# Conv block and MLP in fp32 on one core: the first stage reordered, its matmuls partly in native fp32, TensorE's order pinned, the convolution's DRAM copies issued in separate steps

## The chip, the cores and the metric

The kernel runs on one core of one Trainium2 chip. The metric is the time of one execution in device microseconds (us). Engines are called by the names of the profile: PE (TensorE matmuls), PEld (TensorE weight loads), DVE (VectorE), ACT (ScalarE), POOL (GpSimd), SP (SyncE, which here only issues DMAs). An engine works through its instructions in the order in which they were written for it; a DMA is issued by SP in the same way and then runs on 16 DMA engines.

## The reference

One decoder layer (depth 1) with batch 1, 256 positions (T), width 2048 and an MLP of width 8192, all in fp32. With 16 tiles of 128 channels:

```python
cond = silu(c)
sh1, sc1, g1, sh2, sc2, g2 = split(cond @ mod_w + mod_b, 6)      # mod_w is 2048 x 12288
h = rms_norm(x, norm1_g) * (1 + sc1) + sh1
u = h @ w_in + b_in                                              # 2048 x 4096
u = a * sigmoid(gt), a, gt = split(u, 2)
u = causal depthwise conv, 31 taps, + dw_b
y = silu(layer_norm(u)) @ w_out + b_out                          # 2048 x 2048
x = x + (1 + g1) * y
h = rms_norm(x, norm2_g) * (1 + sc2) + sh2
x = x + (1 + g2) * (square(relu(h @ w1)) @ w2)                   # 2048 x 8192 x 2048
```

## The kernel before

Activations lie with channels on the partitions, so a tile is 128 channels by 256 positions. The weights come from DRAM in blocks of 1024 KB (2048 x 128) into five buffers `raw`; each block is used once. To keep fp32 accuracy at the rate of the type `float32r`, an operand is split into `hi` (its float32r rounding, by ACT) and `lo` (the rest, by DVE or POOL). A product is then hi·hi + hi·lo in one matmul of 512 columns (the activations' hi and lo stand side by side in a tile `hl` or `u2`) and lo·hi in one of 256 columns: L189 and L190 in `mm`, 32 such pairs for an output tile pair, called a job.

The stages, in order:

1. **Start (L86 to L405).** `x` is loaded in four DMAs, squared and summed for the norm's factor `r1`.
2. **Held half (L410 to L487).** The first `HELD` = 7 output tile pairs of `w_in` are accumulated all at once, in seven PSUM banks (`held`), k-tile by k-tile. For each of the 16 k-tiles one block `first` (896 KB, three buffers) is loaded; `split_first` splits it, `first_mm` multiplies it: 14 blocks, three matmuls of 256 columns each (L439, L442, L443). Before k-tile k can be multiplied, its modulation (scale sc1 and shift sh1) must be known, which is a product of `mod_w` with silu(c). It is done in two ways. *By row*: for a group of four k-tiles, eight chunks of 1024 KB (`mod_r`) pass through TensorE (`mod_chunk`, L207, eight matmul records for a chunk), then the row is folded into columns (`mod_finish`, L254). *By column*: for one k-tile, two blocks of 1024 KB (`mod_c`) are multiplied with silu(c) (`cond`) and summed by DVE (`mod_col`, L265). `BY_COL` names the tiles by column (0 to 3 and 12 to 15), `BY_ROW` the groups by row (1 and 2: tiles 4 to 11). The order of k is 0 to 15, so column, row, row, column.
3. **In-stage (L661 to L728).** Jobs 7 to 15 are the other nine tile pairs of `w_in`. After each, `gate` makes the tile `u[i]`. The rest of the modulation goes on as row chunks between the halves of a job (L685, the numbers in `LATE_IN`). The convolution of a channel tile is done by DVE (`conv`, 31 taps, L521), or on TensorE for the tiles in `PE_TILES` (`pe_conv`, L626): there the tile u is copied to DRAM (`flatten`, L594, `flat`), read back in four shifted copies (L611, `wide`, four DMAs for a tile), and multiplied with diagonal 32 x 32 blocks, 64 matmul records for a tile. `CONV_AT` says after which job which tiles are mixed; in job 7 these are 0, 1, 2 and 3. `find_shift` (L288) needs tiles 0 and 1.
4. **Out, up and down jobs (L745 to L815).** Layer norm, `w_out` (8 jobs; `x` is loaded again in four DMAs), then four times 8 up jobs and 8 down jobs. The up jobs read `hl`, the down jobs `u2`, in a pool `mlp` at the upper end of SBUF.

The order of the work on each engine isn't written by hand: a scheduler orders each engine's instructions by its own estimate of when they are ready, and a block under `tc.issue_after(ins)` puts its instructions on `ins`'s engine behind `ins`. `urgent()` raises the priority. The loads follow the list `order`; each goes behind the one before it on SP, and `top_up` issues one more than there are free buffers, so that SP waits for a buffer with everything behind it waiting too.

Of the kernel before, what the change touches and what calls it, by code (L numbers as in the profile page):

```python
# [37 lines left out]
BY_ROW = (1, 2)  # L38
BY_COL = (0, 1, 2, 3, 12, 13, 14, 15)
# [8 lines left out]
CONV_AT = {7: (0, 1, 2, 3), 8: (4,), 9: (5, 6), 10: (7,), 11: (8, 9), 12: (11, 10), 13: (13,), 14: (12,), 15: (14,)}  # L48
SHIFT = 2
UNSHIFTED = 6  # L50
LEAD = {1: 0, 2: 8}
# [13 lines left out]
def conv_block(ctx: ExitStack, tc: tile.TileContext, x, vec, dwq, c_row, mod_r, mod_c, w_first, w_in, w_out, w1, w2, out):  # L65
# [47 lines left out]
    room = {"raw": RAW + 1, "first": FIRST + 1, "cond": 1, "x": 4}  # L113
    todo = []

    def source(key):
# [15 lines left out]
        if kind == "x":  # L132
            return x[:, 4 * key[1] : 4 * key[1] + 4, :]
# [5 lines left out]
    def top_up():  # L139
        while todo and waiting[home(todo[0])] < room[home(todo[0])]:  # L140
# [43 lines left out]
    def mm(p, c, key, acts_of, ks=range(KT)):  # L184
        halves = parts[key]
        for k in ks:
# [3 lines left out]
            nc.tensor.matmul(  # L190
# [123 lines left out]
    def pair_of(tiles, k2):  # L314
        return tiles[k2 // 2][:, 2 * (k2 % 2) : 2 * (k2 % 2) + 2, :]
# [15 lines left out]
    def modulate(k2, r, sh, sc, h):  # L331
        n = scaled(k2, r)
# [32 lines left out]
    order += [("c", 0)]  # L365
    for b in range(4):
        ks = range(4 * b, 4 * b + 4)
        if b in BY_ROW:
            order += first[b] + [("first", k) for k in ks]
        else:  # L370
            for k in ks:
                order += by_col(k) + [("first", k)]
    order += [jobs[HELD] + (c,) for c in range(2)]
    for n, job in enumerate(jobs):
        if n >= HELD and n < len(jobs) - 1:
            order += [jobs[n + 1] + (c,) for c in range(2)]
        if job == ("out", 0):
            order += [("x", i) for i in range(4)]
# [23 lines left out]
    with tc.issue_after(end.ins):  # L402
        mods([("c", 0)])
# [15 lines left out]
    def split_first(k):  # L419
        w = take(("first", k))  # L420
        first_parts[k] = []
# [9 lines left out]
    def first_mm(k):  # L431
        parts_of = first_parts.pop(k)
        m = hl[k // 2][:, k % 2, :]
        for n in range(HELD):
            for c in range(2):
                h, j = divmod(2 * n + c, HELD)
                hi, lo = parts_of[h]
                p = held[n][:, c, :]
                nc.tensor.matmul(  # L439
                    p, hi[:, j, :], m[:, 0:T], start=(k == 0 and c == 0), stop=False, skip_group_check=True  # L440
                )
                nc.tensor.matmul(p, hi[:, j, :], m[:, T : 2 * T], start=False, stop=False, skip_group_check=True)  # L442
                state["step_end"] = nc.tensor.matmul(  # L443
                    p, lo[:, j, :], m[:, 0:T], start=False, stop=(k == KT - 1), skip_group_check=True
# [4 lines left out]
    for b in range(4):  # L449
        ks = range(4 * b, 4 * b + 4)  # L450
        if b in BY_ROW:
            for _ in range(LEAD[b]):
                next(steps, None)
            for at, key in enumerate(first[b]):
                with tc.issue_after(state["step_end"].ins):
                    mods([key])
                with tc.issue_after(state["row_end"].ins):
                    for _ in range(1 + at % 2 if LEAD[b] else 2):
                        next(steps, None)
            mod_finish()  # L460
            for k2 in (2 * b, 2 * b + 1):
                modulate(k2, r1, SH1, SC1, two())
            for k in ks:
                with tc.issue_after(state["fold_end"].ins):
                    for _ in range(2):
                        next(steps, None)
                split_first(k)
            for _ in steps:
                pass
            steps = chain(*(first_mm(k) for k in ks))  # L470
            continue
        for k in ks:
            c = k % 2
            if c == 0:
                n = scaled(k // 2, r1)
                h = two()
                new_hl(k // 2)
            mods(by_col(k))
            nc.scalar.activation(
                h[:, c, :], n[:, c, :], AF.Identity, scale=amps[SC1][:, k : k + 1], bias=mcol(SH1, k)  # L480
            )
            split_act(hl[k // 2][:, c : c + 1, :], h[:, c : c + 1, :])
            split_first(k)
            for _ in steps:
                pass
            steps = first_mm(k)
    for _ in steps:  # L487
        pass
    table(AF.Sigmoid, modc[:, 0:1])
# [105 lines left out]

    def pe_conv(ct, sq=None):
        wide = cp.tile([P, 4, T + 28], F32, name="wide", bufs=2)
        if sq is not None:
            for q in range(4):
                for g in range(4):  # L600
                    dst = wide[32 * q : 32 * q + 32, g, :]
                    src = u[ct][32 * g : 32 * g + 32, q : q + T + 28]
                    if g % 2:
                        nc.vector.tensor_copy(dst, src)
                    else:
                        nc.scalar.activation(dst, src, AF.Copy)
        else:
            src = flats.pop(ct).rearrange("(g c) t -> c g t", g=4)
            with later(ct):
                for q in range(4):  # L610
                    nc.sync.dma_start(wide[32 * q : 32 * q + 32, :, :], src[:, :, q : q + T + 28])  # L611
# [256 lines left out]
```

## Time and profile before

| what | us |
|---|---|
| median of 3 runs (lowest to highest) | 1185.8 (1181.65 to 1187.3) |
| the profiled execution, its own time | 1185.32 |
| its span, first to last instruction | 1183.5 |
| PE busy in the span | 1122.4 |
| DVE, ACT, POOL busy | 744.8, 562.4, 166.1 |
| start and held half: 0 to 146 | 146 |
| in-stage: 146 to 349 | 203 |
| norm and out jobs: 349 to 469 | 120 |
| up and down jobs: 469 to 1178 | 709 |

The stages' limits are read from the timeline of PE. A busy share says only that an engine had an instruction in it; matmul records overlap, so the pitch from one start to the next says more than the length of a record. "SPq" rows are DMA issues by SP; an issue row that is merged over several DMAs includes SP's waits between them.

### The profile page before, as it was taken

The numbers are of one execution on the slowest core, as the hardware profiler recorded it, in microseconds if no ns is written. First come the engines' busy times: TensorE is split into PE (matmuls) and PEld (weight loads), VectorE is DVE, ScalarE is ACT, GpSimd is POOL, SyncE is SP. The second block draws the span as 40 slices with busy tenths as digits, with TensorE's granted clock in tenths as the row PEclk, the third lists the DMA queues.
The fourth block names the chain that finished last, engine by engine and source line by source line (L and its number), as shares of the span: only waits on it lengthen the run. The fifth ranks groups of instructions, "written<-read, shape, count | busy, mean of one in ns | idle before, by whom it ended". The sixth has DMA issues, their size and how long they took to land.

```text
span 1183.5 us, 17371 instructions
## 1 busy us (share of the span) xinstructions
PE 1122.4 (95%) x7048; PEld 931.7 (79%) x7048; DVE 744.8 (63%) x1026; ACT 562.4 (48%) x737; POOL 166.1 (14%) x106
## 2 busy tenths in 40 slices
PE   3879968999989999999999999999999999999998
PEld 3748936666647888888888888888888888888886
DVE  3736899883435886888876555555555655555553
ACT  5234522322347567765443655444555444555441
POOL 0000273664643125200000000000000000000000
PEclk8989988999999999999999999999999999999999
DMA  9998985999977984689777555655555555555630
GB/s 390 401 401 340 414 336 173 356 323 369 305 290 269 342 325 184 222 299 348 285 280 295 194 181 176 213 178 182 200 188 178 192 197 180 182 198 189 197 133 27
DMA packets 46880, 299.81 MB, mean 253 GB/s; under 512 B 5200, under 2 KB 9424, under 8 KB 13520
## 3 DMA queue, kind: packets, MB, share of 16 engines
q1 hardware_dynamic: 46512, 297.99, 68.9%
q8 instruction: 55, 0.90, 0.3%
q10 hardware_dynamic: 288, 0.71, 0.2%
q14 instruction: 25, 0.20, 0.0%
HBM read 295.70 MB, written 2.98 MB: 252 GB/s over the span
## 4 chain that ended last, share of the span: by engine, by line
PE 81%; DMA 3%; SPq 0%; ACT 0%; issue 0%; DVE 0%; POOL 0%; POOLq 0%; ACTq 0%
PE mm L189 50%; PE mm L190 26%; DMA wide<-flat 2%; PE row L207 2%; PE mm L626 2%; DMA raw<-mod_r 1%; PE row L222 0%; SPq L153 0%; PE small L288 0%; PE row L254 0%; PE mm L623 0%; PE small L567 0%; SPq L611 0%; ACT hi L173 0%; ACT sq L340 0%
## 5 line engine op out<-in xcount | busy, mean ns | idle before, releaser
L173 ACT ACTIVATE hi<-raw 128x1024 fp32r<-128x1024 f32 x324 | 342.1, 1059 | 417.3 <-PE mm L189 408.5
L189 PE MATMUL mm<-hl,hi 128*128 128x512 f32 x1504 | 529.4, 396 | 0.2 <-DVE u L639 0.2
L174 DVE TENSOR_TENSOR lo<-raw,hi 128x1024 fp32r<-128x1024 f32 x272 | 333.1, 1226 | 246.0 <-ACT hi L173 244.2
L190 PE MATMUL mm<-hl,lo 128*128 128x256 f32 x1504 | 422.7, 281 | 0.0
L189 PE MATMUL mm<-u,hi 128*128 128x512 f32 x1088 | 384.7, 397 | 0.0
L189 PEld LDWEIGHTS mm<-hl,hi 128*128 128x128 f32 x1504 | 282.2, 188 | 79.6 <-issue 12.1
L190 PE MATMUL mm<-u,lo 128*128 128x256 f32 x1088 | 306.5, 282 | 0.0
L190 PEld LDWEIGHTS mm<-hl,lo 128*128 128x128 f32 x1504 | 284.7, 189 | 5.6 <-issue 5.4
L189 PEld LDWEIGHTS mm<-u,hi 128*128 128x128 f32 x1088 | 204.2, 188 | 50.5 <-DVE small L301 0.2
L190 PEld LDWEIGHTS mm<-u,lo 128*128 128x128 f32 x1088 | 205.1, 189 | 0.0
L174 POOL TENSOR_TENSOR lo<-raw,hi 128x1024 fp32r<-128x1024 f32 x52 | 124.4, 2407 | 99.6 <-ACT hi L173 93.9
L521 DVE SCALAR_TENSOR_TENSOR acc<-u,v,acc 128x256 f32<-128x256 f32 x252 | 107.3, 485 | 2.4
L207 PE MATMUL row<-raw,cz 128*32 128x512 f32 x448 | 61.4, 634 | 16.1 <-DMA raw<-mod_r 15.6
L265 DVE SCALAR_TENSOR_TENSOR raw<-raw 128x2048 f32<-128x2048 f32 x24 | 57.5, 2397 | 14.9 <-DMA raw<-mod_c 14.9
L390 ACT ACTIVATE two<-mm 128x512 f32<-128x512 f32 (+1 forms) x74 | 42.6, 576 | 42.0 <-PE mm L190 41.5
L439 PE MATMUL mm<-hl,hi 128*128 128x256 f32 x128 | 37.4, 303 | 19.9 <-ACT hl L181 19.9
L391 DVE TENSOR_TENSOR two<-mm,two 128x512 f32<-128x512 f32 (+1 forms) x65 | 43.9, 676 | 14.8 <-ACT two L390 13.6
L428 DVE TENSOR_TENSOR lo<-first,hi 128x896 fp32r<-128x896 f32 x32 | 33.9, 1087 | 21.2 <-ACT hi L427 21.2
L439 PEld LDWEIGHTS mm<-hl,hi 128*128 128x128 f32 x128 | 25.2, 202 | 26.6 <-ACT hl L181 21.5
L182 DVE TENSOR_TENSOR u<-two,u 128x512 fp32r<-128x512 f32 x40 | 30.8, 770 | 22.9 <-ACT u L181 22.8
L427 ACT ACTIVATE hi<-first 128x896 fp32r<-128x896 f32 x32 | 28.9, 943 | 25.6 <-DMA first<-w_first 17.4
L442 PE MATMUL mm<-hl,hi 128*128 128x256 f32 x128 | 37.8, 297 | 2.2 <-DVE hl L182 2.2
(138 smaller groups left out, 727.7 us busy)
## 6 DMA issues: line engine op xcount, KB each, us to landing
raw<-w SPq DMA_DIRECT2D x128, 1024.0 KB, 4.9
raw<-mod_r SPq DMA_DIRECT2D x56, 1024.0 KB, 7.8
raw<-mod_c SPq DMA_DIRECT2D x40, 1024.0 KB, 7.3
raw<-w_in SPq DMA_DIRECT2D x18, 1024.0 KB, 8.0
raw<-w_out SPq DMA_DIRECT2D x16, 1024.0 KB, 6.5
first<-w_first SPq DMA_DIRECT2D x16, 896.0 KB, 11.4
x<-x SPq DMA_DIRECT2D x8, 512.0 KB, 7.4
wide<-flat SPq DMA_DIRECT2D x24, 142.0 KB, 9.2
```

Source lines behind the costliest of these rows:

```text
L173: nc.scalar.activation(hi, w[:, ks, :], AF.Copy)
L174: end = engine.tensor_tensor(lo, w[:, ks, :], hi.bitcast(F32), op=ALU.subtract)
L189: nc.tensor.matmul(p[:, c, :], hi[:, k % HALF, :], m, start=(k == 0), stop=(k == KT - 1))
L190: nc.tensor.matmul(p[:, c, T : 2 * T], lo[:, k % HALF, :], m[:, 0:T], start=False, stop=(k == KT - 1), skip_group_check=True,)
L207: state["row_end"] = nc.tensor.matmul(row_ps[0][32 * k : 32 * k + 32, :], cz[:, 4 * kg + k, 3 - b : 35 - b], w[:, 4 * k : 4 * k + 4, :], s ...
L265: nc.vector.scalar_tensor_tensor(w, w, 1.0, cb, op0=ALU.mult, op1=ALU.mult, accum_out=acc)
L390: nc.scalar.activation(t1, p[:, cs, T : 2 * T], AF.Copy)
L391: nc.vector.tensor_tensor(t2, p[:, cs, 0:T], t1, op=ALU.add)
L428: nc.vector.tensor_tensor(lo, w[:, js, :], hi.bitcast(F32), op=ALU.subtract)
L439: nc.tensor.matmul(p, hi[:, j, :], m[:, 0:T], start=(k == 0 and c == 0), stop=False, skip_group_check=True)
L442: nc.tensor.matmul(p, hi[:, j, :], m[:, T : 2 * T], start=False, stop=False, skip_group_check=True)
L521: nc.vector.scalar_tensor_tensor(out, s, w, acc, op0=ALU.mult, op1=ALU.add)
```

## The change

- `BY_ROW` becomes groups 0 and 1, `BY_COL` tiles 8 to 15: the held half now begins with two groups by row and ends with eight tiles by column. The loads are reordered with it: never more than three `first` blocks stand in a row, `c` is loaded behind the rows, and for tiles by column a `first` block comes one tile later.
- Tiles 8, 10, 12 and 14 (`NATIVE`) are not split: TensorE multiplies the fp32 block with the fp32 activation, one fp32 matmul in place of three.
- `LEAD`: six steps of `first_mm` ahead of the second group's chunks, then two steps behind each chunk; `scaled` is called ahead of the chunks.
- `x` is one tile: two loads at the start in place of four, one load later in place of four.
- In the in-stage the row chunks and everything of `mix` get `issue_after` the last matmul of the job so far (`mm_end`).
- The copy to DRAM, the reading back and the convolution are three steps: `flatten` in job i, `widen` in job i + 1 (for the held tiles 0 and 1 right behind the gates), `pe_conv` later. Tiles 0 and 1 move from job 7 to job 8.
- A pad of 64 floats ahead of the pool `mlp` puts `u2` 256 bytes lower.

```diff
-BY_ROW = (1, 2)
-BY_COL = (0, 1, 2, 3, 12, 13, 14, 15)
+BY_ROW = (0, 1)
+BY_COL = range(8, KT)
+NATIVE = (8, 10, 12, 14)
...
-CONV_AT = {7: (0, 1, 2, 3), 8: (4,), 9: (5, 6), ...
+CONV_AT = {7: (2, 3), 8: (0, 1, 4), 9: (5, 6), ...
...
-LEAD = {1: 0, 2: 8}
+LEAD = 6
...
-    xs = [start_pool.tile([P, 4, T], F32, name=f"x{i}") for i in range(4)]
-    for i in range(4):
-        nc.sync.dma_start(xs[i], x[:, 4 * i : 4 * i + 4, :])
+    xs = start_pool.tile([P, KT, T], F32, name="x0")
+    for i in range(2):
+        nc.sync.dma_start(xs[:, 8 * i : 8 * i + 8, :], x[:, 8 * i : 8 * i + 8, :])
...
-                raw[key] = x_pool.tile([P, 4, T], F32, name=f"x{key[1]}")
+                raw[key] = x_pool.tile([P, KT, T], F32, name="x1")
...
-    order += [("c", 0)]
-    for b in range(4):
-        ks = range(4 * b, 4 * b + 4)
-        if b in BY_ROW:
-            order += first[b] + [("first", k) for k in ks]
-        else:
-            for k in ks:
-                order += by_col(k) + [("first", k)]
+    order += first[0] + held_w(0, 1, 2) + first[1][:5] + held_w(3) + first[1][5:] + held_w(4, 5, 6) + [("c", 0)]
+    for k in BY_COL:
+        order += by_col(k) + held_w(k - 1)
+    order += held_w(KT - 1)
...
     def split_first(k):
         w = take(("first", k))
+        if k in NATIVE:
+            first_parts[k] = w
+            return
...
+                if k in NATIVE:
+                    state["step_end"] = nc.tensor.matmul(
+                        p, parts_of[:, j, :], h, start=begin, stop=end, skip_group_check=True
+                    )
+                    continue
...
+    for b in BY_ROW:
+        ks = range(4 * b, 4 * b + 4)
+        pairs = range(2 * b, 2 * b + 2)
+        if b == 0:
+            mods(first[0])
+            ns = [scaled(k2, r1) for k2 in pairs]
+        else:
+            step(LEAD)
+            ns = [scaled(k2, r1) for k2 in pairs]
             for at, key in enumerate(first[b]):
+                if at == 5:
+                    split_first(3)
+                    steps = chain(steps, first_mm(3))
                 with tc.issue_after(state["step_end"].ins):
                     mods([key])
                 with tc.issue_after(state["row_end"].ins):
+                    step(2)
+        mod_finish()
+        for k2, n in zip(pairs, ns):
+            modulate(k2, n, SH1, SC1, two())
+        if b == 0:
+            for k in range(3):
                 split_first(k)
+            steps = chain(*(first_mm(k) for k in range(3)))
+        else:
+            with tc.issue_after(state["fold_end"].ins):
+                for _ in steps:
+                    pass
+            for k in range(4, 7):
+                split_first(k)
+            steps = chain(*(first_mm(k) for k in range(4, 7)))
+    mods([("c", 0)])
+    for k in BY_COL:
...
+        split_first(k - 1)
+        steps = chain(steps, first_mm(k - 1, h_last if k > 8 else None))
+        for _ in steps:
+            pass
+        h_last = h[:, c, :]
...
+    def widen(ct):
+        wides[ct] = cp.tile([P, 4, T + 28], F32, name="wide", bufs=2)
+        src = flats.pop(ct).rearrange("(g c) t -> c g t", g=4)
+        with later(ct):
+            for q in range(4):
+                nc.sync.dma_start(wides[ct][32 * q : 32 * q + 32, :, :], src[:, :, q : q + T + 28])
...
+        for i in range(HELD):
+            if i in PE_TILES:
+                widen(i)
...
                     mm(p, c, job + (c,), hl, ks)
-                    mods(rows[:1])
+                    with tc.issue_after(state["mm_end"].ins):
+                        mods(rows[:1])
...
+            if i - 1 in flats:
+                widen(i - 1)
             if i in PE_TILES and i < KT - 1:
                 flatten(i)
             for ct in CONV_AT.get(n, ()):
-                mix(ct)
+                with tc.issue_after(state["mm_end"].ins):
+                    mix(ct)
...
+            pad = ctx.enter_context(tc.tile_pool(name="pad", bufs=1, side="right"))
+            pad.tile([P, 64], F32, name="pad")
             mp = ctx.enter_context(tc.tile_pool(name="mlp", bufs=1, side="right"))
...
-                xs = [take(("x", n)) for n in range(4)]
+                xs = take(("x", 0))
```

More of the change, by code (lines that the diff above doesn't have):

```diff
@@ L112, in conv_block @@
     waiting = {"raw": 0, "first": 0, "cond": 0, "x": 0}
-    room = {"raw": RAW + 1, "first": FIRST + 1, "cond": 1, "x": 4}
+    room = {"raw": RAW + 1, "first": FIRST + 1, "cond": 1, "x": 1}
     todo = []
@@ L189, in mm @@
             nc.tensor.matmul(p[:, c, :], hi[:, k % HALF, :], m, start=(k == 0), stop=(k == KT - 1))
-            nc.tensor.matmul(
+            state["mm_end"] = nc.tensor.matmul(
                 p[:, c, T : 2 * T], lo[:, k % HALF, :], m[:, 0:T], start=False, stop=(k == KT - 1),
@@ L314, in pair_of @@
     def pair_of(tiles, k2):
+        if tiles is xs:
+            return xs[:, 2 * k2 : 2 * k2 + 2, :]
         return tiles[k2 // 2][:, 2 * (k2 % 2) : 2 * (k2 % 2) + 2, :]
@@ L377, in conv_block @@
         if job == ("out", 0):
-            order += [("x", i) for i in range(4)]
+            order += [("x", 0)]
         order += after[job]
@@ L457, in conv_block @@
                 with tc.issue_after(state["row_end"].ins):
[L458 to L466, printed above, removed]
-                split_first(k)
-            for _ in steps:
-                pass
@@ L470, in conv_block @@
[L470 to L486, printed above, removed]
@@ L488, in conv_block @@
+    split_first(KT - 1)
+    for _ in first_mm(KT - 1, h_last):
         pass
-    table(AF.Sigmoid, modc[:, 0:1])
+    table(AF.Sigmoid, h_last[:, 0:1])
     for c in range(2):
```

70 lines of the change are left out of this document (37 added, 33 removed).

## The prediction, made before the changed kernel was run

> **What bounds the kernel now.** I read the page first: busy shares, the 40 slices, the shares of the chain that ended last.
>
> ```profile
> PE 1122.4 (95%) x7048; PEld 931.7 (79%) x7048; DVE 744.8 (63%) x1026; ACT 562.4 (48%) x737; POOL 166.1 (14%) x106
> ...
> PE   3879968999989999999999999999999999999998
> ...
> PE 81%; DMA 3%; SPq 0%; ACT 0%; issue 0%; DVE 0%; POOL 0%; POOLq 0%; ACTq 0%
> ```
>
> TensorE bounds the kernel. Its 61 us without an instruction (1183.5 − 1122.4) lie in the first 12 slices of 29.6 us, the stages that the change rewrites. The windows show what fills these stages (last two columns: share of the DMA engines, GB/s; before them TensorE's granted clock).
>
> ```profile
> 0.00:140.00 140.00, 109.83 (x799) 91.85 (x800) 82.39 (x113) 56.63 (x80) 0.92 (x6) 0.91 0.95 389
> 100.00:110.00 10.00, 10.00 (x83) 9.81 (x83) 9.21 (x13) 7.44 (x11) 0.00 (x0) 1.00 0.66 258
> 120.00:130.00 10.00, 10.00 (x86) 10.00 (x85) 9.96 (x14) 3.25 (x5) 0.00 (x0) 1.00 1.02 430
> 140.00:350.00 210.00, 190.78 (x1461) 126.24 (x1459) 141.51 (x337) 68.85 (x98) 114.69 (x69) 0.96 0.86 307
> 160.00:170.00 10.00, 2.60 (x23) 0.36 (x16) 10.00 (x26) 2.48 (x3) 8.23 (x5) 0.78 1.02 425
> 205.00:330.00 125.00, 121.80 (x875) 81.17 (x873) 77.09 (x176) 41.86 (x53) 72.00 (x32) 1.00 0.94 338
> ```
>
> Up to 140 us the DMA engines set the pace (0.95 against 1.02 when full), with a hole at 100 to 110. At 160 to 170 TensorE has work for 2.60 us; from 205 on it is full again. TensorE's timeline names the hole.
>
> ```profile
> 146.28 0.50 PE L189 MATMUL mm<-hl,hi 128*128 128x512 f32 x1 [0.23 <-DVE u L639]
> ...
> 155.55 1.06 PE L207 MATMUL row<-raw,cz 128*32 128x512 f32 x8
> ...
> 158.95 1.92 PE L207 MATMUL row<-raw,cz 128*32 128x512 f32 x16
> 161.28 1.06 PE L207 MATMUL row<-raw,cz 128*32 128x512 f32 x8 [0.40 <-DMA raw<-mod_r]
> 169.34 1.93 PE L207 MATMUL row<-raw,cz 128*32 128x512 f32 x8 [7.00 <-DMA raw<-mod_r]
> ...
> 174.21 1.87 PE L207 MATMUL row<-raw,cz 128*32 128x512 f32 x8 [0.50 <-DMA raw<-mod_r]
> 182.26 5.54 PE L626 MATMUL mm<-wide,diag 128*32 128x256 f32 x64 [6.19 <-DMA wide<-flat]
> 188.37 3.66 PE L626 MATMUL mm<-wide,diag 128*32 128x256 f32 x64 [0.57 <-DMA wide<-flat]
> 191.96 0.70 PE L288 MATMUL small<-cv,ones 128*128 128x256 f32 x2
> 192.31 0.58 PE L189 MATMUL mm<-hl,hi 128*128 128x512 f32 x1
> ```
>
> The held half ends at 146.28. Job 7's product follows, then seven row chunks (one at 155.55, two at 158.95, one at 161.28, three from 169.34 to 174.21), two convolutions, the first half of the shift, and only at 192.31 job 8's product. The scheduler had put three chunks of job 8 and both convolutions ahead of that product, and TensorE stood in front of their DMAs. The chain confirms it, and ACT's rows give the marks for the sum: the last held block in, job 7's product out, job 8's product out.
>
> ```profile
> 170.85 8.82 DMA wide<-flat
> 179.69 8.55 DMA wide<-flat
> ...
> 258.30 10.70 DMA wide<-flat
> ```
>
> ```profile
> 136.66 1.79 ACT L427 ACTIVATE hi<-first 128x896 fp32r<-128x896 f32 x2 [4.46 <-DMA first<-w_first]
> ...
> 159.06 0.60 ACT L390 ACTIVATE two<-mm 128x512 f32<-128x512 f32 x1 [5.82 <-PE mm L190]
> ...
> 205.27 0.58 ACT L390 ACTIVATE two<-mm 128x512 f32<-128x512 f32 x1
> ```
>
> **The change part by part.** *Held half, order of loads.* The bytes stay the same, so it can gain only the DMA engines' idle time: 0.07 of 136.66 us (0.95 against 1.02) is 9.6 us. The cause of much of it shows on SP; with it the pace of the held matmuls, and POOL's splits for jobs 7 and 8:
>
> ```profile
> 86.73 15.85 SPq L153 DMA_DIRECT2D first<-w_first  x4
> ...
> 155.97 0.42 SPq L594 DMA_DIRECT2D flat<-u  x1
> ...
> 170.85 2.50 SPq L611 DMA_DIRECT2D wide<-flat  x5
> ...
> 342.85 2.07 SPq L153 DMA_DIRECT2D x<-x  x4
> ```
>
> ```profile
> 143.70 16.56 POOL L174 TENSOR_TENSOR lo<-raw,hi 128x1024 fp32r<-128x1024 f32 x7
> ```
>
> ```profile
> 51.60 0.28 PE L439 MATMUL mm<-hl,hi 128*128 128x256 f32 x1
> 51.72 0.28 PE L442 MATMUL mm<-hl,hi 128*128 128x256 f32 x1
> ```
>
> Four held blocks in a row meet three buffers, and SP waits 15.85 us with the columns behind it; the hole at 100 to 110 follows. In the new order there are at most three in a row, and behind each second-group chunk (about 1 us) stand two steps of six matmuls of 0.12 us (the two starts), 2.4 us together, the pace of one 1024 KB block at 425 GB/s. I take 9.1 us of the 9.6 (bounds 0 and 9.6): nothing in the new order puts a fourth `first` block in line. What is late next is the tail: the last block, its split and its products, 146.28 − 136.66 = 9.6 us as before, since the last tile is still split. So the held half ends at 146.28 − 9.1 = 137.2.
>
> *Native fp32.* The price of a native matmul of 256 columns is in the layer norm's sums:
>
> ```profile
> 345.74 0.59 PE L583 MATMUL mm<-cv,ones 128*128 128x256 f32 x2
> 346.17 0.59 PE L584 MATMUL mm<-sq,ones 128*128 128x256 f32 x2
> ```
>
> A native one is two records and takes 0.43 us from start to start; three split ones take 3 × 0.12 = 0.36. Four tiles of 14 blocks cost 56 × 0.07 = 3.9 us more on TensorE. It is hidden: a tile by column brings 2 × 1024 + 896 KB, some 7.1 us at 425 GB/s, and its products take 5.0 or 6.0 us. Without that cover it costs the 3.9. It takes eight half-block splits off ACT and eight off DVE:
>
> ```profile
> L265 DVE SCALAR_TENSOR_TENSOR raw<-raw 128x2048 f32<-128x2048 f32 x24 | 57.5, 2397 | 14.9 <-DMA raw<-mod_c 14.9
> ...
> L428 DVE TENSOR_TENSOR lo<-first,hi 128x896 fp32r<-128x896 f32 x32 | 33.9, 1087 | 21.2 <-ACT hi L427 21.2
> ```
>
> On DVE 8 × 1.087 = 8.7 us go. A column costs DVE 2.40 us (L265), so a split tile costs 2 × 2.40 + 2 × 1.087 and some 0.8 of small work, 7.8 us, above the 7.1 of its loads, and a native one 5.6. The mean falls below the loads' pace; I count this within the 9.1.
>
> *TensorE's order and the three steps, together.* In jobs 7 and 8 TensorE's work is: two products of 11.8 us (159.06 − 146.28 less one chunk of about 1.0, the first cold pairs included), seven chunks, 7.0, two convolutions at the warm 3.66, 7.3, two sums for the shift, 0.9. Sum 38.8 us, where the timeline needed 205.27 − 146.28 = 59.0. With chunks pinned behind their own half, job 8's product no longer waits for chunks and `wide`; its weights were split by 143.70 + 16.56 = 160.3, and the splits move up with the held half. The copies have more time: `wide` is now issued behind `flat`, not behind the loads that fill 155.97 to 170.85, and is needed only after job 8's product and chunks, at 137.2 + 2 × 11.8 + 7.0 = 168, some 25 us after the gates that follow the held half. SP then waits for `flat` with the next loads behind it; up to five blocks are under way by then, which hide about 12 us of it; without them the wait falls on job 9's weights. I allow 2.1 us, near the lower of the bounds 0 and 13 (the upper one is rival (b)). Job 8's mark: 137.2 + 38.8 + 2.1 = 178.1 in place of 205.27, 27.2 us earlier. Of this 9.1 is the held half, 18.1 the in-stage.
>
> Can the DMA engines follow? From 140 to 350 they idle 0.14 × 210 = 29 us, more than 18.1. And DVE? It is busy 141.5 of these 210 us. So both have room, though the room is used up to a few us.
>
> *The rest of the in-stage.* From 205 to 330 TensorE is busy for 121.8 of 125 us: at most 3.2 us to gain, among them a wait for `wide` at 269; the pinned order may cost as much. I take 0, bounds −3.2 and +5 (a quarter us for each of 21 chunks).
>
> *`x` in fewer DMAs.* Four issues took SP 2.07 us at 342.85, one takes a quarter; the norm is being computed then, so I take 0, bounds −1.6 and +1. At the start the first half lands later, but the sums are not needed before the first group's rows are in: 0, bounds −0.5 and +1.
>
> *MLP buffers 256 bytes lower.* No work changes. The trace gives this question two rows: an up stage (reads `hl`) and a down stage (reads `u2`) with the same instructions.
>
> ```profile
> 670.00:720.00 50.00, 50.00 (x291) 44.10 (x290) 27.34 (x28) 28.24 (x35) 0.00 (x0) 1.00 0.55 190
> 770.00:820.00 50.00, 50.00 (x285) 43.43 (x284) 27.36 (x30) 20.84 (x22) 0.00 (x0) 1.00 0.55 189
> ```
>
> 291 records against 285 in 50 us, TensorE full in both: the pitch differs by 2%. So something that isn't work, possibly where the operand lies, is worth 2% of some 355 us of down jobs, 7 us. I take 0, as the sign is not known, bounds −7 (down jobs as fast as up jobs) and +7 (up jobs as slow). The Trainium skill, page "SBUF — State Buffer", section "SBUF: two separate sides", says that the engines' reads contend only at a port pair shared by VectorE and GpSimd, and that TensorE has ports of its own. By that rule the pad is worth 0, which is also my value; the two rows above don't decide it, but show that equal instructions don't always run at an equal pace.
>
> **Sum.** 9.1 + 18.1 = 27.2 us off the span of 1183.5 gives 1156.3. The profiled execution took 1185.32, 1.8 us beyond its span, so 1158.1; it stands 0.5 below the median of 1185.8. Forecast **1158 us**.
>
> **The rivals.** (a) *The held half doesn't get faster*: another wait takes the place of the four-block queue, for instance first-group products late and their chunks holding `raw`. For it: TensorE and DVE both are near the loads' pace. Then only 18.1 us go: 1167. (b) *`wide` is still late*: SP stays blocked and issues at 170 as before. Convolutions end near 192.3, but job 8's product is done by then: 205.27 − 192.3 = 13.0 us go: 1172. Against it: the issue stands earlier in SP's order. (c) *Down jobs at the up jobs' pace*: 1151. (d) *Up jobs at the down jobs' pace*: 1165. (e) *Slower: the pinned chunks*. In jobs 7 to 14 there are 28 chunks that TensorE may no longer pass. If each comes late by more than 27.2/28 = 0.97 us the gain is gone; at 1.3 us it is 36 lost, some 9 slower: 1195. For it: the DMA share of 0.94 from 205 on, and the 7.00 us wait at 169.34. Against it: chunks stand between products already there, and TensorE is full. (f) *No change*: the stalls reappear in the same sum: 1185. (g) The Trainium skill, page "DMA: Bandwidth & Descriptors", section "Where 436 GB/s comes from", gives about 358 GB/s as the memory's limit for one core. As a mechanism here: loads at 358 in place of 389 GB/s over the first 137 us would end the held half 12 us later and the kernel at 1197; the row of 120 to 130 us, 430 GB/s, is against it. Chance 0.01.
>
> **How the numbers follow.** Chances: forecast 0.41 (its own range 1152 to 1164), (a) 0.10, (b) 0.12, (c) 0.17, (d) 0.08, (e) 0.08, (f) 0.03, (g) 0.01. The range 1146 to 1175 takes in (c) less 5 and (b) plus 3, and leaves out (e), (f), (g) and their like, somewhat over 0.1. A measurement tells about 0.5% (6 us) from no change; the runs before span 0.48%. Faster: 0.41 + 0.10 + 0.12 + 0.17 + 0.08 = 0.88; same 0.03; slower 0.09.
>
> **What would show it.** Right: job 7's first L189 near 137; job 8's L189 at about 153, ahead of any L626; no wait on `wide` above 1 us before 200; job 8's product out near 178; the up and down jobs' record counts unchanged. Wrong: L207 waits of over 1 us on `mod_r` again and again between 150 and 300 (e), L626 waiting for `wide` near 168 (b), L189 near 146 (a), or a changed count for 50 us in the MLP (c, d).

## The result, and the profile after

The changed kernel takes **1166.7 us** (median of 4 runs, 1166.6 to 1168.7), against 1186.6 us of the kernel before on the same chip: a ratio of 0.984 with a 95% interval from 0.981 to 0.988. The forecast was 1158 us, its range 1146 to 1175. So the kernel got faster by about 20 us and not by 27. The profiled execution took 1166.8 us, with a span of 1164.9.

From the page of the kernel after: the busy shares, TensorE's 40 slices and the chain that ended last.

```profile
PE 1125.4 (97%) x6992; PEld 933.1 (80%) x6992; DVE 731.3 (63%) x1018; ACT 555.9 (48%) x730; POOL 167.0 (14%) x106
...
PE   5799999999989999999999999999999999999998
...
PE 84%; DVE 8%; DMA 4%; ACT 2%; issue 1%; POOL 0%; SPq 0%; ACTq 0%; DVEq 0%
```

TensorE's idle time fell from 61 to 39.5 us (1164.9 - 1125.4). The slice with a 6 (at 148 to 178 us) is gone. VectorE, which was on 0% of the chain, is now on 8% of it.

The windows say the same by stage. Columns: TensorE's matmuls, its weight loads, VectorE, ScalarE, GpSimd (busy us and count), granted clock, DMA share, GB/s.

```profile
0.00:140.00 140.00, 115.88 (x763) 95.19 (x764) 75.72 (x106) 51.10 (x74) 0.96 (x7) 0.93 0.97 397
100.00:110.00 10.00, 10.00 (x67) 9.40 (x66) 8.88 (x12) 2.39 (x5) 0.00 (x0) 1.00 0.64 252
140.00:350.00 210.00, 200.21 (x1504) 132.87 (x1503) 146.17 (x355) 85.15 (x127) 125.56 (x77) 0.98 0.91 335
160.00:170.00 10.00, 10.00 (x59) 7.80 (x58) 7.54 (x20) 4.97 (x6) 6.03 (x3) 1.00 1.01 403
205.00:330.00 125.00, 124.45 (x976) 81.48 (x979) 79.11 (x198) 44.08 (x62) 67.79 (x31) 1.00 0.91 330
```

From 160 to 170 us TensorE now works 10.00 us, before 2.60. But the hole of the DMA engines at 100 to 110 us, which the prediction meant to close, is still there (0.64).

TensorE's timeline shows where the gain is and where it isn't.

```profile
145.55 0.50 PE L190 MATMUL mm<-hl,hi 128*128 128x512 f32 x1 [1.92 <-DVE u L668]
...
175.51 3.22 PE L655 MATMUL mm<-wide,diag 128*32 128x256 f32 x54
180.49 1.07 PE L208 MATMUL row<-raw,cz 128*32 128x512 f32 x8 [1.75 <-DMA raw<-mod_r]
181.37 4.50 PE L655 MATMUL mm<-wide,diag 128*32 128x256 f32 x74
186.11 0.70 PE L289 MATMUL small<-cv,ones 128*128 128x256 f32 x2 [0.24 <-ACT cv L660]
```

Job 7's product starts at 145.55, before at 146.28: **the held half gained 0.7 us.** Its last product is through at 143.6, 2.4 us earlier than before, but TensorE then stands 1.92 us for a gate, where it stood 0.23. Then job 8's product runs ahead of both convolutions (L655 is the convolution, L626 before), and the whole set (two products, seven chunks, two convolutions, the first half of the shift) is done at about 186.5, where job 8's product, which then came last of the set, was out at 205.27. From job 7's start that is 40.9 us now and 59.0 before: **the stage of jobs 7 and 8 gained 18 us.** Of these 18.8 us in all, 18.6 arrive at the end of the span.

### The profile page after: what moved, and what is told of

Same layout as the page of the kernel before. It is cut to its first block, busy times and chain, and to the rows that moved or that the text cites. A ratio compares the mean times of both kernels' runs of the same rounds, so it can differ in the third digit from the quotient of the medians.

```text
span 1164.9 us, 17233 instructions
## 1 busy us (share of the span) xinstructions
PE 1125.4 (97%) x6992; PEld 933.1 (80%) x6992; DVE 731.3 (63%) x1018; ACT 555.9 (48%) x730; POOL 167.0 (14%) x106
## 4 chain that ended last, share of the span: by engine, by line
PE 84%; DVE 8%; DMA 4%; ACT 2%; issue 1%; POOL 0%; SPq 0%; ACTq 0%; DVEq 0%
PE mm L190 50%; PE mm L191 25%; PE row L208 3%; DVE raw L266 3%; DVE acc L542 2%; DMA wide<-flat 1%; DVE lo L430 1%; DMA first<-w_first 1%; PE small L289 1%; PE mm L655 1%; DMA raw<-w_in 1%; DMA flat<-u 1%; PE mm L450 1%; PE mm L448 1%; DMA x<-x 1%
## 5 line engine op out<-in xcount | busy, mean ns | idle before, releaser
L190 PEld LDWEIGHTS mm<-hl,hi 128*128 128x128 f32 x1504 | 282.8, 188 | 83.3 <-issue 14.1
L542 DVE SCALAR_TENSOR_TENSOR acc<-u,v,acc 128x256 f32<-128x256 f32 x252 | 102.8, 487 | 0.9
L266 DVE SCALAR_TENSOR_TENSOR raw<-raw 128x2048 f32<-128x2048 f32 x24 | 57.5, 2396 | 33.4 <-DMA raw<-mod_c 33.3
L208 PE MATMUL row<-raw,cz 128*32 128x512 f32 x448 | 60.9, 610 | 10.7 <-DMA raw<-mod_r 10.7
L392 DVE TENSOR_TENSOR two<-mm,two 128x512 f32<-128x512 f32 (+1 forms) x65 | 43.9, 676 | 14.8 <-ACT two L391 13.6
L430 DVE TENSOR_TENSOR lo<-first,hi 128x896 fp32r<-128x896 f32 x24 | 25.4, 1088 | 38.3 <-ACT hi L429 38.3
L448 PE MATMUL mm<-hl,hi 128*128 128x256 f32 x96 | 29.4, 312 | 8.7 <-ACT hl L182 8.7
L266 DVE SCALAR_TENSOR_TENSOR raw<-raw,cond 128x2048 f32<-128x2048 f32 x16 | 36.3, 2286 | 1.8 <-ACT cond L282 1.8
L208 PEld LDWEIGHTS row<-raw,cz 128*32 128x32 f32 x448 | 10.4, 109 | 30.9 <-DMA raw<-mod_r 16.5
L429 ACT ACTIVATE hi<-first 128x896 fp32r<-128x896 f32 x24 | 21.7, 940 | 17.9 <-DMA first<-w_first 16.5
```

What stands on the lines that cost most here:

```text
L190: nc.tensor.matmul(p[:, c, :], hi[:, k % HALF, :], m, start=(k == 0), stop=(k == KT - 1))
L208: state["row_end"] = nc.tensor.matmul(row_ps[0][32 * k : 32 * k + 32, :], cz[:, 4 * kg + k, 3 - b : 35 - b], w[:, 4 * k : 4 * k + 4, :], s ...
L266: nc.vector.scalar_tensor_tensor(w, w, 1.0, cb, op0=ALU.mult, op1=ALU.mult, accum_out=acc)
L392: nc.vector.tensor_tensor(t2, p[:, cs, 0:T], t1, op=ALU.add)
L430: nc.vector.tensor_tensor(lo, w[:, js, :], hi.bitcast(F32), op=ALU.subtract)
L448: nc.tensor.matmul(p, hi[:, j, :], m[:, 0:T], start=begin, stop=False, skip_group_check=True)
```

## The experiments

Each kernel was timed together with the kernel before on its chip (1184.9 to 1185.6 us); ratios are against that. First the change was taken apart.

**In-stage part alone.** The kernel before with the pins, the later place of tiles 0 and 1, and the copies in three steps.

```diff
+CONV_AT = {7: (2, 3), 8: (0, 1, 4), ...
+def widen(ct): ...            # called behind flatten
+with tc.issue_after(state["mm_end"].ins):
     mods(rows[:1])
+with tc.issue_after(state["mm_end"].ins):
     mix(ct)
```

> The kernel before with the in-stage part of the change alone: chunks and mixes pinned behind the last product given out, CONV_AT with tiles 0 and 1 moved to job 8, copies in three steps. The held half, x and the MLP buffers are as before. Theory 1 (the whole gain is made in jobs 7 and 8, and the held half is bound by TensorE from its first product on): job 7's first product still near 146, job 8's product out about 18 us earlier than before, time about 1186.5 - 18 = 1168, within 3 us of the changed kernel's 1166.7. Rival (the new order of the held half is needed, because it is what puts job 8's weights and the copies early enough): at most half the gain, 1177 or more.

Measured: 1171.3 us, ratio 0.989 (0.986 to 0.992), 13.5 us. It gained as much as the whole change up to the norm, and gave some of it back behind it. ScalarE's and TensorE's rows of this kernel: job 8's product out, the last sum of the norm, the first output product.

```profile
173.18 0.60 ACT L390 ACTIVATE two<-mm 128x512 f32<-128x512 f32 x1 [4.54 <-PE mm L190]
```

```profile
328.70 0.59 PE L584 MATMUL mm<-two,ones 128*128 128x256 f32 x2
339.69 0.80 PE L189 MATMUL mm<-hl,hi 128*128 128x512 f32 x1 [6.38 <-DVE hl L182]
```

And the same two marks of the changed kernel:

```profile
329.30 0.59 PE L605 MATMUL mm<-two,ones 128*128 128x256 f32 x2
...
338.15 0.76 PE L190 MATMUL mm<-hl,hi 128*128 128x512 f32 x1 [1.94 <-DVE hl L183]
```

The norm's sums end 0.6 us earlier than in the changed kernel. From there to the first output product it takes 10.4 us (8.3 in the changed kernel), and from that product to the end of the span 1170.0 - 339.7 = 830.3 us (826.8). So Theory 1 holds as far as the norm, and 5.1 us of span differ behind it, which puts the time 3 us over its 1168; two later runs ask why.

**Held half alone.** The changed kernel with the in-stage part and the pad undone.

```diff
-with tc.issue_after(state["mm_end"].ins): ...   # pins
-widen(...)                                     # three steps
-CONV_AT = {7: (2, 3), 8: (0, 1, 4), ...
+CONV_AT = {7: (0, 1, 2, 3), 8: (4,), ...
```

> The changed kernel with the in-stage part undone (no pins, CONV_AT as before, copies in two steps, no pad): what is left is the new order of the held half with its four native tiles, and x in fewer DMAs. Theory 1: job 7's first product at 145 to 146 and the stall in jobs 7 and 8 back, so 1186 and within 3 us of the kernel before. Rival (the held half is worth something that the in-stage part hides or takes back): 1182 or less.

Measured: 1183.5 us, ratio 0.9991 (0.9976 to 1.0006): no difference that can be told. Job 7's product starts at 146.64. All the code moved and rewritten in the first 140 us, four native tiles among it, and `x` in fewer DMAs are worth 1.3 us by the medians, which the interval doesn't tell from nothing. The two parts alone add up to 14.8 us; together they give 18 to 20.

**Pins alone**, and **the two other in-stage edits without pins**:

```diff
 # first kernel: before + pins
+with tc.issue_after(state["mm_end"].ins): ...
 # second kernel: before + CONV_AT + widen, no pins
```

> The kernel before with the pins alone (each row chunk and each mix is given out behind the last product before it). The convolutions of tiles 0 to 3 still stand behind job 7 and wide still comes in two steps. If the pins are what the gain comes from: 1170 or less, job 8's product ahead of any wait for wide. If TensorE's order needs the later place of tiles 0 and 1 as well, because the pin fixes the mixes of tiles 0 and 1 right behind job 7: the wait for wide near 176 to 182 stays ahead of job 8's product, and the time is 1180 to 1190.

> The kernel before with the later place of tiles 0 and 1 and the three steps of the copies, without pins: the scheduler may still put three chunks of job 8 ahead of its product. If waiting chunks were the larger part: 1180 to 1184, TensorE's wait on mod_r of about 7 us near 165 stays. If the convolutions and late copies were the larger part (12.2 of the 20 us, the waits of 6.2 us for wide and the 5.5 us of a convolution that takes them): 1172 to 1176.

Measured: pins alone 1188.6 us, ratio 1.003 (1.0015 to 1.0043), a little slower; the other two edits without pins 1170.7 us, 0.988 (0.986 to 0.990), the same as with them and 1.3 us under the forecast's second case. TensorE's row in the kernel with pins alone:

```profile
179.22 9.93 PE L626 MATMUL mm<-wide,diag 128*32 128x256 f32 x128 [17.85 <-DVE acc L521]
```

and SP's:

```profile
169.44 7.20 SPq L611 DMA_DIRECT2D wide<-flat  x8
```

The mixes of tiles 0 and 1 are pinned behind job 7, so TensorE stands 17.85 us in front of their convolutions. Their `wide` is issued only from 169.44 on and lands 5.2 to 8.5 us after each issue, so for most of the wait it wasn't there; the row names a sum of VectorE's as what came last, and which of the two it was at the end is open. The second kernel shows that nothing needs pinning once they stand later: its job 8's product is out at 172.5.

**The later place alone.**

```diff
-CONV_AT = {7: (0, 1, 2, 3), 8: (4,), ...
+CONV_AT = {7: (2, 3), 8: (0, 1, 4), ...
```

> The kernel before with the later place of tiles 0 and 1 alone: their mixes stand behind job 8 in place of job 7; no pins, copies in two steps as before. If job 8's product stood behind the two convolutions and their wide: most of the 14 us, 1170 to 1174. If the earlier issue of wide is what counts: wide is still issued at the mix, now later than before, TensorE waits for it behind job 8's product, and the gain is under 7 us, 1178 to 1186.

Measured: 1178.0 us, ratio 0.994 (0.992 to 0.996), 7 us: the edge of the second case, and half of the 14. SP's queue and TensorE in this kernel:

```profile
185.22 1.85 SPq L611 DMA_DIRECT2D wide<-flat  x4
187.16 0.68 SPq L153 DMA_DIRECT2D raw<-w_in  x1
187.88 6.59 SPq L611 DMA_DIRECT2D wide<-flat  x4
```

```profile
183.83 1.93 PE L207 MATMUL row<-raw,cz 128*32 128x512 f32 x8 [6.23 <-DMA raw<-mod_r]
...
193.41 1.94 PE L207 MATMUL row<-raw,cz 128*32 128x512 f32 x8 [3.57 <-DMA raw<-mod_r]
...
204.56 3.66 PE L626 MATMUL mm<-wide,diag 128*32 128x256 f32 x64 [1.72 <-DMA wide<-flat]
```

Job 8's product is out at 174.3, 31 us earlier than before, but that alone is not a gain: `wide` is issued only at 185, the second convolution waits for it until 204.56, and TensorE spends the time in front of row chunks. In the kernel with the three steps as well, SP issues `wide` from 160.35 us. The later place is worth some 7 us, and the three steps on top of it another 7. The three steps without the later place were not run, so whether they would gain anything alone is open.

**Pins taken out of the changed kernel.**

```diff
-with tc.issue_after(state["mm_end"].ins):
-    mods(rows[:1])
+mods(rows[:1])                                # the same for mix(ct)
```

> The changed kernel without the pins: row chunks and mixes are given out without regard to the last product. The runs of the kernel before showed pins alone worth nothing (1188.6 against 1184.9) and the rest of the in-stage part worth all of it (1170.7 without pins, 1171.3 with them). If that holds here too: 1166.7 within 2 us. If my own argument holds (the pins are what lets job 8's product pass the chunks): job 8's product behind waits on mod_r again, about 7 us lost, 1174.

Measured: 1167.2 us, ratio 0.984 (0.981 to 0.987): the same as the changed kernel. No gain of the pins can be told.

Now the held half. **Four buffers for held blocks.**

```diff
-FIRST = 3
+FIRST = 4
```

> The changed kernel with four buffers for held blocks in place of three. Theory 1 (TensorE bound, the hole of the DMA engines at 100 to 110 us costs nothing): the hole goes or moves, job 7's first product stays at 145 to 146, 1166.7 within 2 us. Rival (my prediction's view: the DMA engines' idle time is what the held half can gain): the last held block lands near 131 and job 7's first product at 138 to 141, the time 1160 to 1162.

Measured: 1166.9 us, ratio 0.985 (0.983 to 0.987), job 7's product at 146.12. The windows of this kernel and of the changed kernel over the stretch of the columns:

```profile
100.00:110.00 10.00, 10.00 (x66) 9.38 (x65) 8.88 (x11) 2.92 (x5) 0.00 (x0) 1.00 1.01 425
79.00:134.00 55.00, 54.66 (x374) 52.16 (x373) 49.51 (x63) 14.83 (x23) 0.00 (x0) 0.97 1.01 420
```

```profile
79.00:134.00 55.00, 54.47 (x376) 51.90 (x375) 50.08 (x65) 14.47 (x23) 0.00 (x0) 0.99 0.94 391
```

The hole is gone (1.01 in place of 0.64), the DMA engines are full from 79 to 134 us, and the held half ends no earlier. The idle time of the DMA engines, on which the 9.1 us rested, was not what set the pace: TensorE works 54.5 of 55 us with the hole or without it. VectorE doesn't wait for a load in either kernel between 79 and 140 us: all its waits there, 8.8 us, are for ScalarE.

**hl ahead of the weight splits.** In the changed kernel TensorE's first held product waits for ScalarE:

```profile
32.25 1.87 PE L255 MATMUL row<-v,rowsb 128*128 128x2 f32 x8 [0.72 <-ACT rowsb L215]
41.28 0.80 PE L448 MATMUL mm<-hl,hi 128*128 128x256 f32 x2 [7.17 <-ACT hl L182]
```

The rows of the first group are folded at 34 us, and ScalarE splits three weight blocks before it splits the activations. The edit puts the activations first:

```diff
-with tc.issue_after(last_square):
+with tc.issue_after(state["act_end"].ins if "act_end" in state and k < 8 and k != 3 else last_square):
     nc.scalar.activation(hi, w[:, js, :], AF.Copy)
```

> The changed kernel with ScalarE's splits of held blocks 0 to 2 and 4 to 7 put behind the last split of the activations of their group, so that hl is not queued behind weight splits that nobody needs yet. Theory 1 (TensorE starts late, at 41.28 us, and is full from there): its first product of the held half comes about 3 us earlier in each of the two groups, job 7's first product at 140 to 143, the time 1161 to 1164. Rival (loads or VectorE set the end): the earlier start ends in a wait for a column or a block, job 7's first product at 145 to 146, 1166.7 within 2 us.

Measured: 1167.5 us, ratio 0.986 (0.984 to 0.988), and job 7's product at 146.44. TensorE did start earlier, at 37.47 us:

```profile
37.47 0.58 PE L448 MATMUL mm<-hl,hi 128*128 128x256 f32 x1 [4.71 <-ACT hi L429]
```

but it stood still later. Its waits between 79 and 140 us, as the profile groups them (engine and tile, releaser, us in total, times, longest), in this kernel:

```profile
PE mm L450 <- DVE lo L430: 5.2, 3, 2.1
```

in the changed kernel:

```profile
PE mm L450 <- DVE lo L430: 0.5, 1, 0.5
```

The 3.8 us won at the start came back as 4.7 us of waiting for VectorE, whose last column started only 0.6 us earlier (131.16 against 131.78, the last row below); what comes behind it took 1.5 us longer. So Theory 1 as I had put it (TensorE alone) falls. The reason is in VectorE's column sums (L265 before, L266 after), first in the kernel before, then in the changed one; each column is two records:

```profile
0.00:79.00 79.00, 18.25 (x16) 0.85 0.97 394
79.00:146.00 67.00, 18.33 (x16) 1.00 0.93 387
```

```profile
0.00:79.00 79.00, 0.00 (x0) 0.88 0.98 400
79.00:146.00 67.00, 36.38 (x32) 0.99 0.93 386
```

Before, half of the sixteen columns were summed before 79 us, and VectorE was busy for 41.1 of these 79 us. With rows first, all sixteen come behind 79 us: VectorE is busy 22.9 us ahead of that, and 54.2 of the 67 us from 79 to 146, where it was busy 42.7. VectorE's timeline of the changed kernel, the first and the last of them:

```profile
79.75 2.29 DVE L266 SCALAR_TENSOR_TENSOR raw<-raw,cond 128x2048 f32<-128x2048 f32 x1 [1.80 <-ACT cond L282]
...
131.78 2.29 DVE L266 SCALAR_TENSOR_TENSOR raw<-raw,cond 128x2048 f32<-128x2048 f32 x1
```

From 79.75 to 134.1 VectorE needs 54.3 us for the eight tiles, 6.8 us each; then come the last split, its products and the gates, 11.5 us, and job 7's product at 145.55.

**No native tile.**

```diff
-NATIVE = (8, 10, 12, 14)
+NATIVE = ()
```

> The changed kernel with no native tile: all sixteen held blocks are split. Theory 1 (TensorE bounds the held half from 76 us on): its tiles 8, 10, 12, 14 take 5.0 in place of 5.83 us, so job 7's first product at about 142, as long as VectorE can follow. Rival (VectorE becomes the bound): its columns now take 2.2 us more at four tiles, 8.7 us in all, its last column ends near 143 in place of 134 and job 7's first product comes at 149 to 152, the time 1168 to 1172.

Measured: 1170.1 us, ratio 0.988 (0.985 to 0.990), within the rival's range. Job 7's product starts at 146.72, which is 1.2 us later than in the changed kernel and well short of the rival's 149 to 152.

```profile
79.00:134.00 55.00, 50.09 (x387) 49.33 (x386) 54.55 (x70) 20.60 (x30) 0.00 (x0) 0.94 1.00 408
```

Now VectorE is busy 54.55 of 55 us and TensorE waits for it (5.4 us between 79 and 140). VectorE's last column starts 1.8 us later, at 133.54, not 8.7: most of the added work fell into time in which VectorE had waited for ScalarE. The native tiles are worth about 3 us in the new order by the medians, though the runs of the two kernels overlap (1167.2 to 1172.0 against 1166.6 to 1168.7), and only 1.2 us of it shows at job 7's start; where the rest lies was not followed. They hand VectorE's work to TensorE, which is then busy 54.5 of 55 us.

**Several edits at once**, to start the columns earlier, shorten the end and beat the changed kernel:

```diff
-NATIVE = (8, 10, 12, 14)
+NATIVE = (8, 10, 12, 14, 15)
-FIRST = 3
+FIRST = 4
-order += ... first[1][5:] + held_w(4, 5, 6) + [("c", 0)]
+order += ... first[1][5:] + [("c", 0)] + held_w(4, 5, 6)     # and its Silu ahead of their splits
+with tc.issue_after(state["act_end"].ins ...):               # hl first, as above
+with tc.issue_after(state["sg"].ins) ...:                    # weight splits, but job 7's first, behind two gates
```

> The changed kernel with five edits to its held half: hl ahead of the weight splits on ScalarE, as in the run before; c loaded ahead of blocks 4 to 6 and its Silu ahead of their splits; tile 15 native too; four buffers for held blocks; and ScalarE's weight splits for jobs 7 on behind the first two gates. The theory that the earlier runs left: once TensorE starts early, VectorE's sixteen columns in a row set the end (busy from 77.9 to 133.5 us), then the last split, then the gates. By it the columns start 2 to 4 us earlier, the last block needs no split (2.5 us) and the gates' wait of 2 us goes: job 7's first product at 139 to 142 in place of 145.6, and the time 1162 to 1165. Rival (the work behind the held half takes the gain back, as the loads of jobs 7 to 9 are no earlier): job 7's first product early, the time 1166 to 1168. Rival (TensorE's native work takes it): job 7's first product at 145 or later.

Measured: 1166.9 us, ratio 0.984 (0.983 to 0.986), the same as the changed kernel, and job 7's product at 145.64. The third case holds. The columns started only 1.5 us earlier (78.20 against 79.75), because VectorE's six half-block splits for tiles 4 to 6 now came first,

```profile
72.18 6.11 DVE L431 TENSOR_TENSOR lo<-first,hi 128x896 fp32r<-128x896 f32 x6
78.20 2.29 DVE L267 SCALAR_TENSOR_TENSOR raw<-raw,cond 128x2048 f32<-128x2048 f32 x1
```

and at the end TensorE works without a pause through tiles 14 and 15, both native now, about 6 us each, and VectorE's first gate starts only when the last native product is through:

```profile
131.71 3.62 PE L443 MATMUL mm<-two,first 128*128 128x256 f32 x16
...
137.76 3.62 PE L443 MATMUL mm<-two,first 128*128 128x256 f32 x16
...
142.94 1.03 PE L443 MATMUL small<-two,first 128*128 128x256 f32 x4
144.07 0.48 DVE L670 SCALAR_TENSOR_TENSOR u<-mm,v,sg 128x256 f32<-128x256 f32 x1 [8.94 <-PE small L443]
```

In every kernel of this study, old order or new, job 7's product starts between 145.0 and 146.8 us. I found no version that beats the changed kernel by more than the measurement can tell.

**The rest of the change.** The pad, and x in fewer DMAs:

```diff
-pad = ctx.enter_context(tc.tile_pool(name="pad", bufs=1, side="right"))
-pad.tile([P, 64], F32, name="pad")
```

> The changed kernel without the 256-byte pad, so that the MLP's buffers lie where they lay before. My own value for the pad is 0: 1166.7 within 2 us, and 729.7 us from the first down product to the end of the span, as in the changed kernel. By the other theory (where the operand lies sets the pitch of the pairs, worth up to 7 us either way): 1160 or 1174, and a changed count of records in 770 to 820 us.

```diff
 # before + in-stage part, and:
-xs = [start_pool.tile([P, 4, T], F32, name=f"x{i}") for i in range(4)]
+xs = start_pool.tile([P, KT, T], F32, name="x0")
-order += [("x", i) for i in range(4)]
+order += [("x", 0)]
```

> The kernel before with the whole in-stage part and x in fewer DMAs; the held half as before and no pad. The in-stage part alone took 1171.3, the changed kernel takes 1166.7, and the pad is worth nothing. If x in fewer DMAs makes these 4.6 us: 1166 to 1168. If the new order of the held half makes them although job 7's product doesn't come earlier: 1171 within 1.5 us.

Measured: without the pad 1166.6 us, ratio 0.985 (0.983 to 0.988); in-stage part with x 1171.8 us, 0.988 (0.985 to 0.992). Both are worth nothing. So the 4.6 us between the in-stage part alone (1171.3) and the whole change (1166.7) come with the new held half, though it ends no earlier. Most of them lie in the output stage. The row chunks (L207, in the changed kernel L208) from the first output product on, in the kernel with the in-stage part alone, and in the changed kernel:

```profile
339.60:1160.00 820.40, 7.17 (x32) 1.12 (x32) 1.00 0.62 219
```

```profile
338.10:1160.00 821.90, 2.99 (x24) 0.57 (x24) 1.00 0.61 216
```

One chunk more is left, but it costs 4.2 us more, because two chunks stand in five pieces between the products:

```profile
347.34 1.05 PE L207 MATMUL row<-raw,cz 128*32 128x512 f32 x2
...
349.92 1.05 PE L207 MATMUL row<-raw,cz 128*32 128x512 f32 x4
...
359.09 1.04 PE L207 MATMUL row<-raw,cz 128*32 128x512 f32 x2
```

The 7.17 us stand in all three kernels with the old held half and the new steps (with pins, without them, and with x), in no other. So it is an order that the scheduler writes in those kernels, and not a gain in the first 140 us. Why the old held half leads it there was not tried.

## Why the prediction was right, and where it was wrong

- **What bounds it** (TensorE, idle in the first twelve slices): right.
- **Held half, 9.1 us: wrong, measured 0.7 (1.3 us in the time, alone).** The step that failed is the one by which the order of loads "can gain only the DMA engines' idle time", taken as 9.1 of 9.6 us since "nothing in the new order puts a fourth `first` block in line". A fourth block is no longer in line at 86 us, but SP still waits 8.2 us for a buffer until 104.62, until a native tile's last products (L442) give its block free; and with a fourth buffer, which takes the hole away, nothing is gained. Idle DMA engines at 100 us were a mark of a stage paced elsewhere.
- **What sets the held half's end.** The prediction's "Up to 140 us the DMA engines set the pace" is wrong, and the rows of before said so: TensorE is busy 10.00 of 10 us in that hole, and 67.0 of 67 us from 79 to 146. In the changed kernel it is busy 6.6 us more ahead of 79 us (55.4 against 48.8), but 4.1 us more in all up to 146 (2.6 of them the four native tiles' dearer products), and the rest, 2.4 us, it stands idle behind 79 us (0.5 for a split, 1.9 for a gate). What the runs show in place of the DMA engines is TensorE and VectorE close together, with VectorE's columns behind TensorE's waits: those between 79 and 140 us are all for VectorE, more work on VectorE makes the end later, and neither fuller DMA engines nor an earlier TensorE makes it earlier. The converse, columns that end well earlier and job 7 with them, no run shows, so that VectorE alone would set the end is argued. I had the columns' price right (7.8 and 5.6 us a tile, mean 6.7; measured 6.8) and compared it with the loads' 7.1, but did not ask when the first of the eight tiles can start and what VectorE does until then. The measured end is the first column's start, eight tiles and what comes behind them, 79.75 + 54.3 + 11.5 = 145.6; the first and the last of these are read from the trace of after, and whether the rows of before would have given them was not tried.
- **Native fp32, hidden:** its price is about right (from first product to the next tile's first, a native tile takes 5.86 us and a split one 5.22; the prediction had 6.0 and 5.0), the cover isn't: TensorE is busy 54.5 of 55 us there. It is paid for by VectorE's 8.7 us, and without it the kernel is some 3 us slower by the medians.
- **Jobs 7 and 8, 18.1 us: right, measured 18** (40.9 us for the set of work, as the sum 38.8 + 2.1 says). **But the mechanism credited first is wrong:** the prediction has job 8's product pass because chunks are "pinned behind their own half". The pins are worth nothing in three pairs of runs. The later place of tiles 0 and 1 and, on top of it, the earlier issue of `wide` make the gain, some 7 us each. Two of the signs hold for the reason given: job 8's product runs ahead of any convolution, and there is no wait on `wide` above 1 us before 200. That this product is out at 175.6, near the forecast 178, is luck: 178.1 is the prediction's sum for the whole set of work, and by its own words the two products and the chunks would be done at 168. The set is done at 186.5, and these 8.4 us are the ones that the held half didn't gain. The 2.1 us allowed for SP show as a wait of 1.75 us for a row chunk (at 180.49).
- **Nothing given back later:** about right for the whole change (the norm's last sum starts at 329.30 in place of 348.76, 19.5 us earlier, and the span ends 18.6 earlier), but by luck: the in-stage part alone has 20.1 us at that mark and 13.5 in the span, and gives back 6.6.
- **x and the pad, 0 each:** right, and the up and down jobs' record counts are unchanged (rows at the end). The rule of the Trainium skill, page "SBUF — State Buffer", section "SBUF: two separate sides", by which the pad is worth 0, agrees with the runs (1166.6 without, 1166.7 with it). Rivals (c) and (d) fall with it.
- **DMA rate:** with a fourth buffer the loads ran at 420 GB/s over 55 us, so rival (g) is not what happened. The figure behind it, about 358 GB/s for one core by the Trainium skill, page "DMA: Bandwidth & Descriptors", section "Where 436 GB/s comes from", doesn't agree with these runs on one core.
- **The rivals.** (a) is what happened: it named TensorE and VectorE near the loads' pace and gave 1167; the measured time is 1166.7, outside the forecast's own 1152 to 1164. Its example, late products of the first group, is not what bound the stage: with these 3.8 us earlier nothing was gained. It had a chance of 0.10, the forecast 0.41. The same sentence stood as an argument for it, "TensorE and DVE both are near the loads' pace"; with three engines at nine tenths or more, a gain on one of them should have been the rival's case and not the forecast's.

## What to carry to other kernels

Where three engines are busy to nine tenths in the same stage, the idle time of one of them need not be a gain to be had: work out for each engine when its first piece of work can start, add its whole work and its tail, and take the latest. An order of loads also sets when each engine's share begins; moving all of one engine's work (here the columns) behind a point takes away the time in which it was free. When a stall is removed by several edits together, take them apart, since the edit that reads like the cause (the pins) can be the idle one.

## What the runs showed of the hardware

- A row chunk is four matmuls of 128*32 and takes 1.06 us when they follow each other; a piece of one or two of them between other products takes 1.05 us just as well (rows above). Broken up, two chunks cost 5.2 us in place of 2.1.
- A native fp32 product over 14 blocks costs TensorE 5.86 us against 5.22 us for the split one with three matmuls per block (changed kernel, starts at 98.38, 104.24 and 109.46, granted clock 1.00).
- The 2% between up and down stages is not a matter of these 256 bytes. An up and a down stage in the changed kernel, and in the one without the pad (windows, columns as above):

```profile
650.00:700.00 50.00, 50.00 (x290) 44.10 (x290) 27.43 (x27) 27.86 (x35) 0.00 (x0) 1.00 0.55 190
745.00:795.00 50.00, 50.00 (x285) 43.40 (x284) 29.46 (x33) 20.78 (x23) 0.00 (x0) 1.00 0.54 182
```

```profile
650.00:700.00 50.00, 50.00 (x290) 44.06 (x289) 27.92 (x27) 28.01 (x35) 0.00 (x0) 1.00 0.56 190
745.00:795.00 50.00, 50.00 (x285) 43.45 (x284) 28.94 (x33) 21.54 (x23) 0.00 (x0) 1.00 0.54 182
```

The counts are the same with the buffers 256 bytes lower or not; its cause stays open.
